# Weights of the feed-forward and of two layers in scaled float16 parts instead of float32r parts

## The chip, the cores and the metric

The kernel runs on one core of one Trainium2 chip. The metric is the device time of one launch in microseconds, the median of several launches. Five engines matter: TensorE (PE) multiplies, its stationary operand being loaded by a separate step (PEld); VectorE (DVE) and ScalarE (ACT) work elementwise and are the ones that read TensorE's results out of PSUM; GpSimd (POOL) does small statistics; SyncE (SP) issues most DMAs. Each runs its own instructions in order and waits for the others on semaphores.

## The reference, cut to what matters

One decoder block over 512 tokens of width 1024, then two mixer layers over the same tokens and 256 context tokens, all in float32:

```python
h = rms_norm(x, norm_ffn_g)                       # end of the first block
x = x + jnp.square(jax.nn.relu(h @ w_ff1)) @ w_ff2

for i in range(2):                                # the two layers
    hx = rms_norm_2(x, g_pre) * (1.0 + scale_x) + shift_x
    hc = rms_norm_2(ctx, g_pre) * (1.0 + scale_c) + shift_c
    ... = in_proj(hx, w_in), in_proj(hc, w_in)    # 7200 columns
    ya = window_attn_latent(...)                  # branch a
    yb = mla_attn_latent(...)                     # branch b, over w_qb and w_kvb
    yc = short_gated_conv(...)                    # branch c
    m = (sigmoid(ga) * ((ya * silu(za)) @ w_branch[0])
       + sigmoid(gb) * ((yb * silu(zb)) @ w_branch[1])
       + sigmoid(gc) * ((yc * silu(zc)) @ w_branch[2]))
    x = x + gate_x * rms_norm_2(m @ w_o, g_post)
```

Ahead of the feed-forward the first block has a projection, a sparse attention with compressed keys, a spatial gating unit and a cross attention to 256 memory tokens; this is called the front here.

## The kernel before

Precision comes from two parts. Each float32 operand is split into a high part in float32r and a low part (the rest, also float32r), and a product is made as three matmuls in `mm3` (L291 to L293): high by high, high by low, low by high, added up in PSUM. The moving operand has up to 512 columns.

Weights go through `Stream` (L147 on). SyncE loads chunks of 1024 columns into three rotating raw tiles; a chunk is two units of 512 columns; for each unit ScalarE writes the high part `wh` (L182) and VectorE the low part `wl` (L183) into a ring of nine such units. `pump` makes the next unit whenever the ring has room; `get` makes it at once if a product needs it. The ring is refilled as products release units.

The program is a list of operations written out by hand: for each product a block of weights (`wblk`) and a generator that yields its cost after each step. A driver (`tick`) runs them in order, pumps the ring, lets chains of dependent steps (norms, rotations, transposes) go on when their time is due, and mixes background attention in at a fixed rate. The framework then orders each engine's instructions.

`form_a` multiplies with tokens on the output partitions (weights move), `form_b` and the first feed-forward product with features on the output partitions (tokens move, 512 columns for x, 256 for the context). The stages, with their start in the profile:

- 0 us: the front. Its last part is w_mo's product and two blocks of modulation weights (`mod`).
- about 457: the feed-forward in eight chunks of 512 hidden columns, `ff1` and `ff2`; blocks of modulation weights stand between some.
- about 843: layer 0. Products KA and QA, then branch a's attention in the background of branch c's products (`conv`: CC, UC, BC, ZC).
- about 1105: KL and QL, then branch b's attention. ZA's products, the gate of branch a in pieces (`agate`), stand ahead of it and between its items as fillers.
- about 1349: `merge`, four steps for each branch in the order c, a, b; a step multiplies by its gate's weights and by w_branch. `zgate` (ZB, branch b's gate) stands ahead of b's merge. Then w_o.
- about 1768: layer 1, the same without context outputs.

Branch values go to DRAM and come back (`y_load`), each split into float32r parts. Norms take six small steps on POOL (`rstd`, L279 to L287). In branch attention the probabilities and values are float16 or bfloat16 parts already.

## Time and profile before

| | |
|---|---|
| Three launches | 2448.72, 2451.61, 2451.70 us; median 2451.61 |
| Span of the profiled execution, first to last instruction | 2444.0 us |
| Matmuls in it | 14268, listed busy 2352.0 us |
| VectorE, ScalarE, POOL busy | 1458.1, 1123.3, 208.7 us |
| Mean granted TensorE clock | 0.988 of full |

The profile is of one execution; its span leaves out what lies around the instructions of the program, and that execution's own launch time is not listed beside it. A matmul's listed duration includes its pipeline's tail, which overlaps the next matmul; the spacing of starts is what each costs in a stream. Half clock was granted only in a dozen short stretches, most in the front and at the starts of the stages.

### The profile page before, as it was taken

To read this page: it belongs to the slowest core of one execution; us is meant where nothing else is said; L and a number is where in the kernel's file an instruction comes from. 1 tells how busy PE (TensorE), PEld (TensorE's weight loads), DVE (VectorE), ACT (ScalarE), POOL (GpSimd) and SP (SyncE) were. 2 spreads that over 40 slices of the span, in tenths; PEclk is the share of its full clock that TensorE was granted. 3 is DMA by queue.
4 is the path that set the end of the run, shared out by engine and by line. 5 is a ranking of instruction groups with operands and counts; after the bars stand their busy time and mean duration, and the time that the engine had idled before them with its cause. 6 is when DMAs were issued, how large, how long until landed. Compare 5 with 4: busy or idle time off the path is not lost. (4 is left out here: it accounts for less than half of the span.)

```text
span 2444.0 us, 37374 instructions
## 1 busy us (share of the span) xinstructions
PE 2352.0 (96%) x14268; PEld 1971.2 (81%) x14268; DVE 1458.1 (60%) x2772; ACT 1123.3 (46%) x2461; POOL 208.7 (9%) x574
## 2 busy tenths in 40 slices
PE   7899899999999999999999999999989999999998
PEld 6777687777788888889888888888878798888886
DVE  5878668655544667664677423443577657863444
ACT  5656457543333345434576322322445556752332
POOL 4310321200000100003000000000400020000001
PEclk9999999999999999999999999999999999999999
DMA  4512445533532311212212321222422223133332
GB/s 156 131 54 70 156 129 171 150 121 121 164 104 86 121 52 46 63 36 62 80 49 78 119 61 54 81 70 78 137 79 61 63 61 107 44 109 90 104 95 95
DMA packets 182247, 226.63 MB, mean 93 GB/s; under 512 B 28588, under 2 KB 130908, under 8 KB 182068
## 3 DMA queue, kind: packets, MB, share of 16 engines
q1 hardware_dynamic: 158116, 187.67, 25.8%
q10 hardware_dynamic: 23952, 36.57, 4.5%
q8 instruction: 112, 1.84, 0.3%
q14 instruction: 67, 0.55, 0.1%
HBM read 207.33 MB, written 16.88 MB: 92 GB/s over the span
## 5 line engine op out<-in xcount | busy, mean ns | idle before, releaser
L182 ACT ACTIVATE wh<-raw 128x512 fp32r<-128x512 f32 (+4 forms) x668 | 401.8, 618 | 454.3 <-PE mm L292 223.6
L183 DVE TENSOR_TENSOR wl<-raw,wh 128x512 fp32r<-128x512 f32 (+4 forms) x668 | 437.7, 673 | 201.7 <-ACT wh L182 194.1
L291 PE MATMUL mm<-hTh,wh 128*128 128x512 f32 (+1 forms) x1040 | 415.2, 400 | 2.0 <-ACT wh L182 1.2
L292 PE MATMUL mm<-hTl,wh 128*128 128x512 f32 (+1 forms) x1040 | 410.6, 395 | 0.0
L293 PE MATMUL mm<-hTh,wl 128*128 128x512 f32 (+1 forms) x1040 | 409.5, 394 | 0.0
L293 PEld LDWEIGHTS mm<-hTh,wl 128*128 128x128 f32 x1040 | 196.3, 189 | 45.1
L291 PEld LDWEIGHTS mm<-hTh,wh 128*128 128x128 f32 x1040 | 196.5, 189 | 44.7 <-ACT wh L182 1.6
L292 PEld LDWEIGHTS mm<-hTl,wh 128*128 128x128 f32 x1040 | 196.8, 189 | 40.9
L568 ACT ACTIVATE ph<-mm 128x512 f16<-128x512 f32 (+2 forms) x300 | 147.7, 503 | 148.9 <-PE mm L564 132.7
L569 DVE SCALAR_TENSOR_TENSOR pl<-mm,ph 128x512 f16<-128x512 f32 (+2 forms) x300 | 166.9, 567 | 73.7 <-ACT ph L568 70.5
L291 PE MATMUL mm<-wh,hTh 128*128 128x512 f32 (+4 forms) x512 | 186.4, 366 | 4.6 <-ACT wh L182 1.9
L293 PE MATMUL mm<-wh,hTl 128*128 128x512 f32 (+4 forms) x512 | 185.3, 362 | 0.0
L292 PE MATMUL mm<-wl,hTh 128*128 128x512 f32 (+4 forms) x512 | 184.9, 363 | 0.0
L564 PE MATMUL mm<-ident,P 128*128 128x128 f32 x928 | 148.8, 278 | 3.7 <-ACT P L551 1.8
L279 POOL TENSOR_SCALAR s<-s 128x1 f32<-128x1 f32 (+4 forms) x89 | 35.4, 397 | 1116.5 <-ACT xn L444 949.1
L551 ACT ACTIVATE P<-S,s 128x768 f32<-128x768 f32 (+4 forms) x160 | 106.0, 667 | 30.1 <-PE mm L564 16.3
L564 PEld LDWEIGHTS mm<-ident,P 128*128 128x128 f32 x928 | 106.4, 142 | 14.9 <-ACT P L551 3.6
L1897 ACT ACTIVATE z<-mm 128x256 f32<-128x256 f32 (+1 forms) x72 | 37.4, 519 | 170.1 <-PE mm L293 170.1
L291 PEld LDWEIGHTS mm<-wh,hTh 128*128 128x128 f32 x512 | 98.0, 192 | 17.2 <-ACT wh L182 2.3
L291 PE MATMUL mm<-hch,wh 128*128 128x256 f32 x384 | 110.8, 289 | 0.5 <-DVE y L1646 0.4
L1904 DVE SCALAR_TENSOR_TENSOR z<-z,mm 128x512 f32<-128x512 f32 (+1 forms) x48 | 28.8, 599 | 134.7 <-PE mm L293 134.4
L293 PE MATMUL mm<-hch,wl 128*128 128x256 f32 x384 | 109.0, 284 | 0.0
(473 smaller groups left out, 5347.2 us busy)
## 6 DMA issues: line engine op xcount, KB each, us to landing
raw<-in_w_in_dram SPq DMA_DIRECT2D x124, 512.0 KB, 3.7
raw<-in_w_ff_dram SPq DMA_DIRECT2D x64, 512.0 KB, 3.9
raw<-in_w_mod_dram SPq DMA_DIRECT2D x48, 512.0 KB, 3.8
raw<-in_w_branch_dram SPq DMA_DIRECT2D x24, 512.0 KB, 3.3
raw<-in_w_o_dram SPq DMA_DIRECT2D x16, 512.0 KB, 3.8
raw<-in_cmp_w_dram SPq DMA_DIRECT2D x16, 256.0 KB, 3.6
raw<-in_w_out_dram SPq DMA_DIRECT2D x8, 512.0 KB, 4.4
raw<-in_w_mkv_dram SPq DMA_DIRECT2D x8, 512.0 KB, 4.8
```

The lines of the kernel that those rows point to most:

```text
L182: nc.scalar.activation(hi[:, :m], src, AF.Copy)
L183: nc.vector.tensor_sub(lo[:, :m], src, hi[:, :m].bitcast(FT))
L279: POOL.tensor_scalar(a, ms, EPS, None, op0=OP.add)
L291: PE.matmul(ps, ah, bh, start=start, stop=False)
L292: PE.matmul(ps, ah, bl, start=False, stop=False)
L293: PE.matmul(ps, al, bh, start=False, stop=stop)
L551: ACT.activation(P, v[:, j, :], AF.Exp, bias=it.nb[:, j:j + 1], accum_out=it.den[:, j:j + 1])
L564: PE.transpose(ps[:, a - a0, :], it.P[0 if len(it.P) == 1 else j][:, c:c + 128], ident)
L568: ACT.activation(ph[:, :m], ps[:, :m], AF.Copy, scale=PSC)
L569: DVE.scalar_tensor_tensor(pl[:, :m], ps[:, :m], PSC, ph[:, :m], op0=OP.mult, op1=OP.subtract)
L1897: ACT.activation(th[sg], ps, AF.Tanh, scale=0.5)
L1904: DVE.scalar_tensor_tensor(th[sg], th[sg], 1.0, ps, op0=OP.add, op1=OP.mult)
```

## The change

All weight products of the feed-forward and, in the layers, those of w_in and w_branch take two float16 parts instead of two float32r parts; the number of matmuls of these products and their shapes stay. The front, the modulation weights, w_qb, w_kvb and w_o keep float32r (`fr=True`). Float16 has a narrow range, so:

- Weights get a scale for each group of blocks (a feed-forward step's two blocks, a gate with its w_branch, two of conv's blocks, or a single block). `stat` squares each raw chunk on ScalarE with its sums kept, up to four chunks ahead; `scale` and `total` add the sums over partitions by a one-column matmul and take the power -0.5 on POOL. Only then can a group's parts be made.
- A unit is now 1024 columns, the ring still nine units. The high part is a scaled copy on ScalarE, or on POOL where `pool=True` (conv, KL, QL, ZA); the low part is one VectorE instruction for each 512 columns, emitted one pump later (`finish`).
- Norm gains and the layers' scale and shift are scaled once, branch values by a scale from their own squares (`ystat`, `yscale`); the products are multiplied back where they leave PSUM (`unscale`, argument `c` or `u`).
- The token tiles `hTh`, `hTl` become two halves each. After the memory query product float16 tiles take the first halves and the second halves become four more raw tiles; two more come from the space of memory attention's output. So there are three raw tiles in the front and nine after.
- The last ZA block's pieces (two in layer 0, one in layer 1) move from branch b's attention to the start of `merge`; ZB moves from ahead of b's merge to ahead of a's. Branch b's gated values stay on the chip until they are split.

```diff
 class Stream:
...
+    def stat(self, lo):
...
+        for a in range(0, m, w):
+            b = min(m, a + w)
+            nc.scalar.activation(lo[:, :b - a], t[:, a:b], AF.Square, accum_out=g.t[:, g.cols:g.cols + 1])
...
+        if g.seen == g.total:
+            self.full.append((self.state.clk, g))
...
+    def pump(self, must=False):
...
+        while self.full and self.full[0][0] + LAG <= self.state.clk:
+            self.scale()
...
+        n = 1 if self.ns < 4 else 2
+        while n and self.nstat < self.nd and self.nstat <= ci + AHEAD:
+            n -= self.stat(lo)
...
+        elif fr:
             nc.scalar.activation(hi[:, :m], src, AF.Copy)
             nc.vector.tensor_sub(lo[:, :m], src, hi[:, :m].bitcast(FT))
         else:
...
+            s = g.t[:, G_S:G_S + 1]
+            if u.blk.pool:
+                nc.gpsimd.tensor_scalar(hi[:, :m], src, s, 1.0, op0=OP.mult, op1=OP.mult)
+            else:
+                nc.scalar.activation(hi[:, :m], src, AF.Copy, scale=s)
...
+    def finish(self):
...
+            for a in range(0, l.shape[-1], 512):
+                b = slice(a, min(a + 512, l.shape[-1]))
+                self.nc.vector.scalar_tensor_tensor(l[:, b], src[:, b], s, h[:, b], op0=OP.mult, op1=OP.subtract)
...
+    def total(ss, s, i):
+        b = sbp.tile([128, 2], BF, tag="sb", name="sb")[:, 0:1]
+        with nc.allow_low_precision(reason="a scale need not be exact"):
+            DVE.reduce_sum(b, ss, axis=AX)
+        ps = trtile(1)
+        PE.matmul(ps[:, 0, 0:1], onesb.to_broadcast([128, 128]), b, start=True, stop=True)
+        DVE.tensor_scalar(i, ps[:, 0, 0:1], 2.0 ** -30, 1e-30, op0=OP.mult, op1=OP.max)
+        POOL.tensor_tensor(s, i, neghalf[:, 0:1], op=OP.pow)
+        DVE.reciprocal(i, s)
...
+    def hT16():
+        for i, p in enumerate("hl"):
+            H[p] = one.tile([128, 8, 512], F16, tag=f"H{p}0", name=f"hT{p}")
+            more_raw(f"H{p}1")
...
         for n, b in enumerate((2, 0, 1)):
             if n == 0:
                 add(lambda: yc_load(nn))
-            elif n == 2:
+                for n2 in range(behind, len(pieces)):
+                    f, sg = pieces[n2]
+                    add(lambda *b, n2=n2: piece(n2), *([za[f]] if sg == segs[0] else []))
+                add(lambda: ya_load(nn))
+            elif n == 1:
+                g = Group()
                 for f2 in range(2):
                     add(lambda bl, f2=f2: zgate(f2, segs, bl, yb_d, nn),
-                        wblk(w[:, ZB + f2 * 256:ZB + (f2 + 1) * 256]))
+                        wblk(w[:, ZB + f2 * 256:ZB + (f2 + 1) * 256], g))
```

How this orders the engines, at three places. First TensorE at the start of the feed-forward: `ms` are the modulation's vectors, `xn` a normed token tile to be transposed, `sb` a group's sums, `hTh` and `hTl` the tokens' parts. Before:

```order
L1267 MATMUL mm<-wh,ms_616 34x512
L460 MATMUL S<-ident,xn 128x128 x8
L1268 MATMUL mm<-wl,ms_616 2x512
...
L291 MATMUL mm<-hTh,wh 128x256
L292 MATMUL mm<-hTl,wh 128x256
...
L1270 MATMUL mm<-wh,ms_616 34x512
...
L293 MATMUL mm<-hTh,wl 128x256
```

Now:

```order
L1447 MATMUL mm<-wh,ms_618 34x512
L430 LDWEIGHTS onesb
L430 MATMUL S<-sb,onesb 128x1
...
L416 LDWEIGHTS wh
L416 MATMUL mm<-hTh,wh 128x256
L417 LDWEIGHTS wh
L417 MATMUL mm<-hTl,wh 128x256
```

Each float16 matmul has its own load instruction, where a float32r matmul carries it within, and two sums over partitions stand ahead of the first product.

Second ScalarE at the same place: `z` is the first product on its way out, `raw` a chunk of weights, `gs` a group's sums and scale. Before:

```order
L182 ACTIVATE wh<-raw 128x512 x2
L296 ACTIVATE hTh<-S 128x4x128
L1215 ACTIVATE z<-mm 128x256 x2
L182 ACTIVATE wh<-raw 128x512
L1216 ACTIVATE z<-z 128x256 x2
```

Now:

```order
L421 ACTIVATE hTh<-S 128x4x128
L224 ACTIVATE wl,gs<-raw 128x1024
L1451 ACTIVATE z<-mm 2x512
L224 ACTIVATE wl,gs<-raw 128x1024
L273 ACTIVATE wh<-raw,gs 128x1024 x8
...
L224 ACTIVATE wl,gs<-raw 128x1024 x2
L1392 ACTIVATE z<-mm 128x256
```

Copies of 512 columns became a square (with the low part's tile as its scratch) and a scaled copy, of 1024 columns each.

Third POOL at the start of layer 0, where the six steps of `rstd` for x's token tiles stand (`s`). Before:

```order
L279 TENSOR_SCALAR s_8955<-s_8953 128x1
L281 TENSOR_TENSOR s_8957<-s_8955,nh 128x1
L283 TENSOR_TENSOR s_8959<-s_8957 128x1
L284 TENSOR_TENSOR s_8959<-s_8959,s_8955 128x1
L285 TENSOR_SCALAR s_8959<-s_8959 128x1
```

Now:

```order
L404 TENSOR_SCALAR s_8948<-s_8946 128x1
L406 TENSOR_TENSOR s_8950<-s_8948,nh 128x1
L271 TENSOR_SCALAR wh<-raw,gs 128x1024
L408 TENSOR_TENSOR s_8952<-s_8950 128x1
L271 TENSOR_SCALAR wh<-raw,gs 128x1024
L409 TENSOR_TENSOR s_8952<-s_8952,s_8948 128x1
L410 TENSOR_SCALAR s_8952<-s_8952 128x1
```

Copies of weights for conv now stand between the steps of a norm; one more stands ahead of the norm before it.

## Rows read from the trace of the kernel before

**Rows 1.** The page: span, and busy time, share and instructions by engine.
```profile
span 2444.0 us, 37374 instructions
PE 2352.0 (96%) x14268; PEld 1971.2 (81%) x14268; DVE 1458.1 (60%) x2772; ACT 1123.3 (46%) x2461; POOL 208.7 (9%) x574
```

**Rows 2.** Stretches: us, engines' busy us (instructions), granted clock, DMA share, GB/s.
```profile
0.00:457.00 457.00, 415.93 (x2996) 332.90 (x2997) 343.45 (x634) 271.53 (x619) 113.32 (x294) 0.97 0.41 125
457.00:843.00 386.00, 384.46 (x1747) 308.64 (x1747) 206.31 (x324) 150.90 (x260) 13.74 (x32) 1.00 0.39 123
843.00:1105.00 262.00, 255.58 (x1773) 221.94 (x1772) 167.10 (x399) 118.89 (x290) 1.95 (x7) 0.99 0.18 51
...
1349.00:1768.00 419.00, 415.95 (x2285) 358.42 (x2284) 167.01 (x260) 119.39 (x220) 26.49 (x63) 1.00 0.27 84
```

**Rows 3.** Timeline, TensorE, merge: start, duration, engine, line, operation; float32r.
```profile
1408.81 0.40 PE L291 MATMUL mm<-hTh,wh 128*128 128x512 f32 x1
...
1417.23 0.28 PE L291 MATMUL mm<-hch,wh 128*128 128x256 f32 x1
...
1420.08 0.28 PE L291 MATMUL mm<-yh,wh 128*128 128x256 f32 x1
```

**Rows 4.** Timeline, TensorE: first and last of two runs of 16-bit matmuls.
```profile
163.92 0.27 PE L983 MATMUL O<-Vd,ph 128*128 128x256 bf16 x1
...
164.91 0.27 PE L987 MATMUL O<-Vd,pl 128*128 128x256 bf16 x1
...
1343.66 0.22 PE L585 MATMUL O<-ph,vb 128*128 128x128 f16 x1 [0.48 <-DVE yb L1794]
...
1344.78 0.22 PE L585 MATMUL O<-ph,vb 128*128 128x128 f16 x1
```

**Rows 5.** Groups by line and shape: count, busy us, mean ns, idle before.
```profile
L182 ACT ACTIVATE wh<-raw 128x512 fp32r<-128x512 f32 x620 | 380.7, 630 | 434.6 <-PE mm L292 208.2 <-PE mm L293 82.2 <-DVE oc L1067 50.8
L551 ACT ACTIVATION_READ_ACCUMULATOR P<-S,s 128x1 f32 x160 | 32.6, 203 | 0.0
L444 ACT ACTIVATE xn<-oc 128x1024 f32<-128x1024 f32 x12 | 12.6, 1053 | 12.4 <-DVE oc L1067 10.8 <-POOL s L284 1.6
L183 DVE TENSOR_TENSOR wl<-raw,wh 128x512 fp32r<-128x512 f32 x620 | 415.5, 688 | 188.4 <-ACT wh L182 181.1 <-PE mm L564 4.7 <-PE mm L292 1.0
L539 DVE TENSOR_TENSOR nb<-s,sk 128x1 f32<-128x1 f32 x64 | 9.6, 151 | 0.6
L512 DVE SCALAR_TENSOR_TENSOR vb<-xn,s,vb 128x512 f16<-128x512 f32 x6 | 4.4, 747 | 0.1
L501 POOL TENSOR_TENSOR s<-s,nh 128x1 f32<-128x1 f32 x6 | 3.6, 607 | 206.5 <-DVE s L500 206.5
```

**Rows 6.** Groups by line and shape, POOL: its two widest kinds.
```profile
L876 POOL COPY Vd<-v 32x384 bf16<-32x384 bf16 x4 | 2.1, 525 | 17.6 <-DVE v L874 17.5
L1253 POOL MEMSET xn<- 128x1024 f32 x1 | 1.0, 952 | 0.0
```

**Rows 7.** Timeline, the first microseconds, VectorE and POOL.
```profile
7.70 0.22 POOL L279 TENSOR_SCALAR s<-s 128x1 f32<-128x1 f32 x1 [6.52 <-ACT xn L444]
...
9.70 1.28 DVE L448 SCALAR_TENSOR_TENSOR xn<-x,s,g 128x1024 f32<-128x1024 f32 x1 [2.71 <-POOL s L287]
9.75 1.31 POOL L279 TENSOR_SCALAR s<-s 128x1 f32<-128x1 f32 x1
```

**Rows 8.** Waits (total us, times, longest): feed-forward twice, then merge.
```profile
PE mm L291 <- ACT wh L182: 1.2, 1, 1.2
...
ACT wh L182 <- PE mm L293: 68.3, 10, 8.5
...
PE mm L291 <- ACT yh L296: 2.6, 1, 2.6
```

**Rows 9.** Timeline, TensorE at the start of layer 0.
```profile
843.14 1.06 PE L460 MATMUL S<-ident,xn 128*128 128x128 f32 x8
848.01 1.30 PE L460 MATMUL S<-ident,xn 128*128 128x128 f32 x5 [3.81 <-DVE xn L450]
```

More of the change, by code (lines that the diff above doesn't have):

```diff
@@ L157, in __init__ @@
         self.ns = 0
-        self.done = 0
+        self.nstat = 0
         self.live = 0
+        self.full = []
+        self.half = None
     def loads(self):
-        while self.nd < len(self.chunks) and self.nd - self.done < RAWB:
-            dmas, _ = self.chunks[self.nd]
-            t = self.rawp.tile([128, 1024], FT, tag="raw", name="raw")
+        while self.nd < len(self.chunks) and self.slots:
+            dmas, us = self.chunks[self.nd]
+            t = self.slots.pop(0)
             for dst, src in dmas:
@@ L275, in decoder_kernel @@
     POOL.memset(onesf, 1.0)
+    onesb = one.tile([128, 1], BF, tag="onesb", name="onesb")
+    POOL.memset(onesb, 1.0)
     def rstd(ms, n, p=128):
@@ L410, in decoder_kernel, with more_raw @@
     prevb = one.tile([128, 128], BF, tag="prevb", name="prevb")
[L412 to L413 removed]
+    H = {p: Halves(*[one.tile([128, 4, 512], FR, tag=f"H{p}{i}", name=f"hT{p}") for i in range(2)]) for p in "hl"}
+    def hT16():
+        for i, p in enumerate("hl"):
+            H[p] = one.tile([128, 8, 512], F16, tag=f"H{p}0", name=f"hT{p}")
+            more_raw(f"H{p}1")
+    def more_raw(tag):
+        t = one.tile([128, 2, 1024], FT, tag=tag, name="raw")
+        stream.slots += [t[:, 0], t[:, 1]]
+        stream.loads()
     def hA(t, k):
@@ L1330, in s23_start @@
         open_scope(f"s{i}")
+        rot["kd"] = Rot(sc["kd"], "kd", 2, 256)
         lay["i"] = i
+        lay["ih"] = f"l{i}"
+        lay["yss"] = [small(8) for _ in range(3)]
+        lay["yn"] = dict.fromkeys("abc", 0)
         one2 = sc["one"]
-        ra = one2.tile([128, 384], FT, tag="ra", name="ra")
+        ra = one2.tile([128, 384], FT, tag="yb", name="ra")
         nc.scalar.dma_start(out=ra, in_=c_ra)
@@ L2154, in decoder_kernel @@
     layer(1)
-    stream = Stream(nc, rawp, ringp, [b for blks, _ in ops for b in blks])
+    slots = [one.tile([128, 1024], FT, tag=f"raw{i}", name="raw") for i in range(3)]
+    stream = Stream(nc, slots, ringp, scalep, total, D, [b for blks, _ in ops for b in blks])
     stream.loads()
```

446 lines of the change are left out of this document (297 added, 149 removed).

## The prediction, made before the changed kernel ran

> **What bounds the kernel now.** I read the page's busy times first, then a table of stretches, then the spacing of matmuls in the timeline, then the waits. TensorE is busy 96% of the 2444.0 us span [rows 1]. That word needs care: a 128x512 matmul is listed with 0.39 to 0.40 us, but the next one starts after 0.23 us, so "busy" also covers a tail that overlaps its successor. What counts is the spacing. In a clean run of the merge stage 36 matmuls with 512 float32r columns start within 8.42 us, 233.9 ns apart, and the 24 with 256 columns behind them within 2.85 us, 118.8 ns apart [rows 3]. In the feed-forward stretch (386 us) and in the merge stretch (419 us) the matmuls simply follow one another; TensorE is busy all but 1.5 and 3 us there, VectorE and ScalarE about half the time or less [rows 2]. The waits say who leads: in the feed-forward ScalarE's split of weights waits 68.3 us for a matmul (a ring slot that is still being read), while matmuls wait 1.2 us for that split [rows 8]. Weights are ready ahead of their use, so in these stretches the time is the number of matmuls times their spacing. In the front (0 to 457) TensorE has 41 us without work, on chains of dependent steps; the change hardly enters there.
>
> **What float16 does to the spacing.** The trace of before has 16-bit matmuls, each with a load of its own 128x128 stationary tile as the changed ones will have: ten with 256 columns start within 0.99 us, 9 spacings of 110 ns, and 21 with 128 columns within 1.12 us, 20 of 56 ns [rows 4]. So 128 more columns cost 54 ns, and 512 columns come to 110 + 2 x 53 = 216 ns (estimate; twice the 256-column spacing gives 220, the longest). Against 233.9 that is 17.9 ns less for each matmul; for 256 columns 118.8 - 110 = 8.8, up to 9.7 with the rounding of the rows; I take 9.3. Per column both are 0.035, which gives 10 ns for 288 and 13.5 for 384 columns.
>
> The counts follow from the loops. Feed-forward: 8 chunks x (96 + 96) = 1536, of which 48 are split in two halves of 256 columns. Layer 0: 1584 with 512 columns (merge 864, conv 384, ZA 96, ZB 96, QA 144), the same number with 256 (context; KA for QA), 144 with 288, 144 with 384. Layer 1: 1536 with 512, 144 with 256, 144 with 288, 96 with 384. Together 4608 x 17.9 = 82.5, 1824 x 9.3 = 17.0, 288 x 10 = 2.9 and 240 x 13.5 = 3.2: **105.6 us less TensorE work.** Nothing in TensorE's work for the front, the attention products, the modulation, qb, kvb and w_o changes.
>
> **What it adds.**
> - On TensorE: 74 one-column products for sums (66 weight groups, 2 modulations, 6 branch sums). No row shows one; between nothing (it slips behind a wait) and the 56 ns of [rows 4], I take 56: 4.1 us.
> - On ScalarE, for each 1024 columns of weights: before, two copies of 630 ns; after, a square of 1053 with its sum (203) and one scaled copy of 1053 [rows 5], 1.05 us more. In the feed-forward 64 x 1.05 = 67 us on top of 150.9, 218 of some 359 us, 61%. It stays beside the matmuls and I cost it at nothing; without that cover it would be 67.
> - On VectorE the low parts: 2 x 747 (a scalar_tensor_tensor with float16 output) for 2 x 688 [rows 5], 0.12 us more for each chunk, 8 us in the feed-forward, plus some five small instructions of 0.15 for each group: nothing on the path, with 206 of 386 us busy there [rows 2].
> - At each group a chain: the last square's sum 0.20, a reduce 0.15, the product, a VectorE step 0.15, POOL's power 0.61, a reciprocal and the factor 0.3, the scaled copy 1.05, two low parts 1.49: some 4.0 us [rows 5]. The ring holds nine units of 1024 columns behind it (before: nine of 512), each worth some 24 matmuls x 216 ns = 5 us, and nine raw tiles stand for four chunks of a group. So it is hidden, except where a ring starts empty of scaled parts: ahead of the first feed-forward product, where four squares (4 x 1.26 = 5.0) come before the chain (4.0). Between 0 and 9 us; 4 taken, since slots for these loads open a whole attention earlier.
> - On POOL: high parts of conv, KL, QL and ZA, 27 chunks for each layer. No row shows POOL reading 1024 columns. A memset of 1024 takes 952 ns, a copy of 384 bfloat16 columns 525 ns [rows 6]; from 0.95 to 384-column pace x 1024 = 1.4 us, and twice that if its two operations are done one after the other: 1.4 taken, as the row that reads. Two things queue behind them. First the norms at the start of a layer: in the order on POOL a copy stands before x's norm and two more between steps of the next one. TensorE waits 3.81 us there for exactly such a norm [rows 9], so up to 3 x 1.4 = 4.2 for each layer; 4 taken, 8 in all. Second VectorE in conv: its low part now waits for a POOL copy instead of a ScalarE copy of 0.63, and attention's reductions are queued behind it. VectorE is busy 167 of 262 us there and TensorE has only 6 us without work [rows 2]. Between 0 and 16 chunks x 1.4 = 22 us a layer; 4 taken for each, 8 in all, nearer to none because VectorE has a third of its time free.
> - With one answer, nothing: the gains scaled once (two VectorE passes over 1024 columns, in the memory block), the factor on the way out of PSUM (the same instructions with another operand, one more on VectorE in branch c's merge), the squares of branch values on ScalarE (0.6 each beside matmuls), the narrower tiles of the front's compression, the same DMAs in number of bytes. Each hides beside matmuls on an engine with free time.
> - Moved: layer 0's two and layer 1's one last ZA piece go from branch b's attention to the start of merge, ahead of branch c's first use. TensorE waited 2.6 us there for yh [rows 8]; the pieces (24 x 216 and 24 x 110 ns, 7.8 us) cover that. Attention loses the same filler, about a wait of 1 us each. I take 2 us less for both layers together. ZB, moved one merge earlier, has its sum ready a whole merge ahead and costs nothing.
>
> **A rule against it.** A POOL instruction on one column that took 0.22 us at 7.70 lasts 1.31 us at 9.75, just as long as VectorE's two-input instruction that began at 9.70 [rows 7]. The Trainium skill ("SBUF — State Buffer", Who interferes with whom) states the rule: POOL and VectorE share a pair of ports under an exclusive lock, held for the whole instruction, when POOL reads SBUF and VectorE has two SBUF inputs. The trace agrees, and the rule speaks against this part of the change: it says that the new copies stop VectorE's low parts too. What that makes of the sum is the first rival.
>
> **Sum.** -105.6 + 4.1 + 4 + 8 + 8 - 2 = -83.5. The span falls from 2444.0 to 2360.5. Launches were timed at a median of 2451.61, 7.6 us above the profiled span; with the same 7.6 I get **2368 us**, 3.4% less. A measurement of this kernel can tell about 0.2% from no change, some 5 us.
>
> **Rivals.**
> 1. POOL and VectorE block one another in conv and the lat stage. Then each of the 54 copies costs up to its own 1.4 and the 0.69 of a low part it waits for, 2.1 x 54 = 113 us if all of it lay on the path. VectorE's free third says most does not; with a third exposed 38 us instead of my 16: 2390, and up to 2410. For it: [rows 7] and the norms at a layer's start. Against it: the ring's depth.
> 2. Everything added is hidden and the longer ring and nine raw tiles take up waits as well: -105.6 + 4.1 - 4 = -105.5, 2346; with 512 columns at 214 ns another 9 less, 2337. For it: TensorE barely waits for weights now [rows 8].
> 3. It doesn't do what it says at 512 columns: 16-bit matmuls of that width keep 234 ns, because what holds them is not the operand width. No 16-bit row has 512 columns. Then only the narrower ones gain, -23.1 + 22.1 = -1.0: 2451, no change. Against it: 56 and 110 ns lie on a straight line through nearly no fixed cost.
> 4. Slower: the group chain is not hidden. If units of a group become ready only after TensorE has used up the ring, each of 66 groups exposes 4.0 us, 264 us; it decides from 105.6 / 66 = 1.6 us exposed for each group, and in full gives 2444 - 105.6 + 264 + 22 + 7.6 = 2632. For it: no part can be made before the last chunk of its group has landed and been squared. Against it: the ScalarE waits of 68.3 us for slots [rows 8] show supply well ahead.
>
> **How the numbers follow.** Forecast (2355 to 2382) 0.66; rival 1 (2383 to 2415) 0.13; rival 2 (2335 to 2354) 0.12; rival 3 (2440 to 2456) 0.03; rival 4 (above 2457) 0.06. Faster 0.91, same 0.03, slower 0.06. The range takes the forecast, rival 2 and most of rival 1: 2337 to 2406.
>
> **What would show it.** In the changed profile: the spacing of 512-column matmuls in feed-forward and merge 214 to 218 ns (right) or 234 (rival 3); the feed-forward stretch about 386 - 27 = 359 us long; layer 0's merge, from 1349 to 1768, 26 us shorter but for the 7.8 us of the moved pieces; matmuls waiting for wh or wl hardly more than before (otherwise rival 4, with ScalarE's squares or POOL's power as releasers); POOL copies of wh near 1.4 us, and VectorE's waits for wh in conv short (long ones, and a conv stretch no shorter than 262 us: rival 1); at a layer's start TensorE's wait for the norm 4 us longer; at the start of merge no wait for the branch. I am wrong if TensorE's clock falls more often than before, or if ScalarE or VectorE is the one that TensorE waits for in the feed-forward.

## The result and the profile after

The changed kernel takes 2423.26 us (median of four launches, 2421.47 to 2425.71) against 2451.19 for the kernel before on the same chip: a ratio of 0.9886, 95% interval 0.9872 to 0.9900. It is faster by 28 us (1.1%), a third of the forecast 83.5, and the time lies above the forecast range. The profiled execution has a span of 2419.7 us, against 2444.0 in [rows 1].

The page of the changed kernel, span and busy time by engine:

```profile
span 2419.7 us, 38066 instructions
PE 2261.3 (93%) x14342; PEld 1505.2 (62%) x14342; DVE 1544.2 (64%) x3136; ACT 1298.1 (54%) x2745; POOL 320.7 (13%) x703
```

TensorE's busy time fell by 91 us, so its work did shrink; ScalarE gained 175 us and VectorE 86. The spacing of matmuls is what was forecast. The timeline of TensorE in layer 0's merge (start, duration, engine, line, operation):

```profile
1384.75 0.38 PE L416 MATMUL mm<-hTh,wh 128*128 128x512 f16 x1
...
1389.93 0.38 PE L416 MATMUL mm<-yhl,wh 128*128 128x512 f16 x1
...
1392.52 0.27 PE L416 MATMUL mm<-hc,wh 128*128 128x256 f16 x1
...
1395.14 0.27 PE L416 MATMUL mm<-yhl,wh 128*128 128x256 f16 x1
```

24 matmuls with 512 columns start within 5.18 us, then 12 within 2.59, both 215.8 ns each; 24 with 256 columns within 2.62, 109 ns each. The number of matmuls by width is as counted in the prediction, so some 105.6 us of TensorE work did go. Where the time came back shows in the stretches. First the kernel before, from the feed-forward on, then the changed kernel (length, then busy us and instructions of TensorE, its weight loads, VectorE, ScalarE and POOL, then the granted clock, the DMA share and GB/s). The four of before are the feed-forward, branch b's attention in layer 0, and layer 1's two stretches ahead of merge:

```profile
457.00:833.00 376.00, 374.46 (x1662) 298.71 (x1663) 197.17 (x312) 144.71 (x248) 11.28 (x25) 1.00 0.39 122
...
1109.00:1349.00 240.00, 228.54 (x1688) 206.53 (x1687) 167.08 (x351) 147.95 (x378) 22.29 (x74) 0.99 0.22 65
...
1761.00:1976.00 215.00, 201.73 (x1328) 167.17 (x1326) 151.58 (x338) 105.87 (x245) 11.56 (x28) 0.98 0.27 79
1976.00:2165.00 189.00, 182.47 (x1348) 162.24 (x1347) 141.28 (x296) 125.04 (x310) 18.51 (x62) 0.99 0.23 64
```

```profile
469.00:821.00 352.00, 347.81 (x1666) 162.80 (x1665) 213.92 (x394) 204.94 (x334) 21.18 (x39) 0.99 0.42 134
...
1090.00:1332.00 242.00, 219.22 (x1649) 176.61 (x1648) 170.92 (x382) 164.95 (x415) 30.86 (x85) 0.98 0.23 69
...
1726.00:1961.00 235.00, 194.02 (x1337) 126.19 (x1336) 174.05 (x389) 113.62 (x265) 51.73 (x66) 0.95 0.25 75
1961.00:2153.00 192.00, 177.31 (x1320) 140.59 (x1318) 143.90 (x326) 137.88 (x336) 27.13 (x73) 0.98 0.24 72
```

The feed-forward lost 24 us of 27 forecast, but it starts 12 us later (469 instead of 457). In branch b's attention TensorE is busy 9 us less, and the stretch is 2 us longer. In layer 1's first stretch it is busy 8 us less, and the stretch is 20 us longer. The same as a table, by the first matmul of each stage in the traces (us, the last stage up to its last matmul; "L0 a" is layer 0 to the end of branch a's attention and conv, "L0 b" branch b's attention, "merge" with w_o). The other rows are the experiments below:

| kernel | front | feed-forward | L0 a | L0 b | merge 0 | L1 a | L1 b | merge 1 |
|---|---|---|---|---|---|---|---|---|
| before | 456.9 | 375.8 | 276.8 | 239.4 | 411.9 | 215.2 | 188.7 | 271.2 |
| changed | 468.9 | 352.3 | 268.8 | 241.7 | 394.1 | 235.2 | 192.4 | 257.9 |
| constant scale, squares kept | 457.4 | 373.6 | 271.5 | 240.4 | 393.4 | 231.9 | 193.3 | 256.4 |
| constant scale, no squares | 454.2 | 362.8 | 267.4 | 232.2 | 389.4 | 224.4 | 184.2 | 256.3 |
| the same, units of 512 | 450.2 | 355.4 | 264.1 | 224.8 | 391.8 | 210.2 | 181.9 | 258.0 |
| the same, ring of eighteen | 453.4 | 362.8 | 266.7 | 233.9 | 390.9 | 227.5 | 187.2 | 257.9 |

The stages in which TensorE runs from one matmul to the next (merge) gained what was forecast: 17.8 us for layer 0, where 26 less the 7.8 of the moved pieces was expected. Of the stages with chains of dependent steps only layer 0's first gained, 8.0 us; the other three became 2 to 20 us longer.

### The profile page after: what moved, and what is told of

Same layout as the page of the kernel before. It is cut to its first block, busy times and chain, and to the rows that moved or that the text cites. A ratio compares the mean times of both kernels' runs of the same rounds, so it can differ in the third digit from the quotient of the medians.

```text
span 2419.7 us, 38066 instructions
## 1 busy us (share of the span) xinstructions
PE 2261.3 (93%) x14342; PEld 1505.2 (62%) x14342; DVE 1544.2 (64%) x3136; ACT 1298.1 (54%) x2745; POOL 320.7 (13%) x703
## 5 line engine op out<-in xcount | busy, mean ns | idle before, releaser
L416 PE MATMUL mm<-hTh,wh 128*128 128x512 f16 (+1 forms) x1040 | 392.6, 378 | 7.3 <-ACT wh L273 3.1
L291 DVE SCALAR_TENSOR_TENSOR wl<-raw,gs,wh 128x512 f16<-128x512 f32 (+2 forms) x420 | 296.6, 751 | 150.6 <-ACT wl L224 116.5
L417 PE MATMUL mm<-hTl,wh 128*128 128x512 f16 (+1 forms) x1040 | 392.4, 377 | 0.0
L418 PE MATMUL mm<-hTh,wl 128*128 128x512 f16 (+1 forms) x1040 | 391.2, 377 | 0.0
L224 ACT ACTIVATE wl<-raw 128x1024 f16<-128x1024 f32 (+3 forms) x242 | 222.9, 921 | 69.6 <-PE mm L417 37.3
L416 PEld LDWEIGHTS <-wh 128*128 128x128 f16 x1712 | 168.0, 98 | 147.4 <-issue 6.8
L417 PEld LDWEIGHTS <-wh 128*128 128x128 f16 x1712 | 168.0, 98 | 146.1 <-issue 9.6
L273 ACT ACTIVATE wh<-raw,gs 128x1024 f16<-128x1024 f32 x156 | 175.3, 1141 | 105.9 <-PE mm L417 83.0
L416 PE MATMUL mm<-wh,hTh 128*128 128x512 f32 (+5 forms) x512 | 181.7, 356 | 5.5 <-DVE vf L1589 2.0
L418 PE MATMUL mm<-wh,hTl 128*128 128x512 f32 (+5 forms) x512 | 180.1, 352 | 1.8 <-DVE hTl L422 1.7
L417 PE MATMUL mm<-wl,hTh 128*128 128x512 f32 (+5 forms) x512 | 180.1, 352 | 0.3 <-DVE wl L267 0.3
L271 POOL TENSOR_SCALAR wh<-raw,gs 128x1024 f16<-128x1024 f32 (+3 forms) x54 | 65.8, 1219 | 328.2 <-PE mm L417 209.9
```

What stands on the lines that cost most here:

```text
L224: nc.scalar.activation(lo[:, :b - a], t[:, a:b], AF.Square, accum_out=g.t[:, g.cols:g.cols + 1])
L273: nc.scalar.activation(hi[:, :m], src, AF.Copy, scale=s)
L291: self.nc.vector.scalar_tensor_tensor(l[:, b], src[:, b], s, h[:, b], op0=OP.mult, op1=OP.subtract)
L416: PE.matmul(ps, ah, bh, start=start, stop=False)
L417: PE.matmul(ps, ah, bl, start=False, stop=False)
L418: PE.matmul(ps, al, bh, start=False, stop=stop)
```

## What the waits say

TensorE's waits in branch b's attention of layer 0 (total us, times, longest), before and then changed:

```profile
PE S L291 <- ACT P L551: 3.2, 4, 1.4
```

```profile
PE S L416 <- ACT P L721: 12.1, 11, 2.5
```

A score waits for an exponential nine microseconds more. ScalarE's timeline in one of these waits shows what stood ahead of it:

```profile
1263.62 1.13 ACT L273 ACTIVATE wh<-raw,gs 128x1024 f16<-128x1024 f32 x1
...
1264.66 1.04 ACT L224 ACTIVATE wl<-raw 128x1024 f16<-128x1024 f32 x1
1265.61 0.19 ACT L224 ACTIVATION_READ_ACCUMULATOR wl<-raw 128x1 f32 x1
1265.70 0.61 ACT L1862 ACTIVATE qb<-y 128x512 fp32r<-128x512 f32 x1
1266.34 0.87 ACT L738 ACTIVATE ph<-mm 128x512 f16<-128x512 f32 x2
1267.10 0.91 ACT L721 ACTIVATE P<-S,s 128x768 f32<-128x768 f32 x1
```

A scaled copy of one chunk and the square of another, with its sum, take 2.1 us without a break (1263.62 to 1265.70), and the exponential P comes behind them. Not all of the 2.1 us is P's delay: it needs the largest score of each row, and VectorE takes that until 1264.94:

```profile
1263.99 0.95 DVE L705 TENSOR_REDUCE s<-S 128x1 f32<-128x768 f32 x1
```

From then on some 0.8 us of the square are left, and 1.4 us of `qb` and `ph`, which the square had held up as well. ScalarE is busy 165 of 242 us in this stretch, 68%, so there is room on average; but the engine runs its instructions in order, and here the weights' stand ahead of the exponential. What the changed kernel spends on scaled copies (L273, L271) and on statistics (L224) is in its groups by line and shape (count, busy us, mean ns, idle before):

```profile
L273 ACT ACTIVATE wh<-raw,gs 128x1024 f16<-128x1024 f32 x156 | 175.3, 1141 | 105.9 <-PE mm L417 83.0 <-POOL gs L432 22.6
L224 ACT ACTIVATE wl<-raw 128x1024 f16<-128x1024 f32 x164 | 171.5, 1046 | 61.0 <-PE mm L417 35.6 <-PE mm L418 12.6 <-DVE ffh L1394 5.3
L271 POOL TENSOR_SCALAR wh<-raw,gs 128x1024 f16<-128x1024 f32 x40 | 53.0, 1328 | 222.0 <-PE mm L417 127.6 <-PE mm L418 69.1 <-issue 24.4
L224 ACT ACTIVATION_READ_ACCUMULATOR wl<-raw 128x1 f32 x242 | 45.6, 188 | 0.0
L224 ACT ACTIVATE wl<-raw 128x512 fp32r<-128x512 f32 x64 | 39.7, 620 | 1.9 <-PE mm L417 1.7
```

A square also uses the low part's tile as scratch, so that VectorE's low part must wait for it. In branch b's attention of layer 0 that is not what costs; VectorE waited 0.7 us for squares there:

```profile
L291 DVE SCALAR_TENSOR_TENSOR wl<-raw,gs,wh 128x512 f16<-128x512 f32 x23 | 16.3, 746 | 1.9 <-POOL wh L271 1.2 <-ACT wl L224 0.7
```

The second place is the start of layer 1. VectorE, POOL and TensorE in the changed kernel:

```profile
1741.55 6.57 DVE L291 SCALAR_TENSOR_TENSOR wl<-raw,gs,wh 128x512 f16<-128x512 f32 x6
1748.04 0.20 DVE L311 TENSOR_SCALAR gs<-gs,ih 128x1 f32<-128x1 f32 x1
1748.17 1.40 DVE L291 SCALAR_TENSOR_TENSOR wl<-raw,gs,wh 128x512 f16<-128x512 f32 x2
1749.49 0.74 DVE L2196 SCALAR_TENSOR_TENSOR xt<-ob,s,xt 128x512 f32<-128x512 f32 x1
```

```profile
1741.42 0.19 POOL L410 TENSOR_SCALAR s<-s 128x1 f32<-128x1 f32 x1
1741.59 4.67 POOL L271 TENSOR_SCALAR wh<-raw,gs 128x1024 f16<-128x1024 f32 x3
1746.22 0.62 POOL L412 TENSOR_TENSOR s<-s,s 128x1 f32<-128x1 f32 x1
```

```profile
1750.80 0.69 PE L1581 MATMUL S<-ident,kd 128*128 128x128 f32 x2 [8.64 <-ACT kd L1556]
```

Eight low halves stand in a row ahead of `xt`, w_o's result going into x, on which the norms and, by the profile's waits, `kd` depend; TensorE stands still for 8.64 us. Six of the halves take 1.10 us each instead of the 0.70 of the last two, while POOL makes three copies. These copies also stand between the last two steps of the norm that `xt` needs (L410 and L412), so `xt` could not start before 1746.84: for the first 4.7 us either of the two would have held it, for the last 2.6 the low halves alone do. Four theories follow: statistics load ScalarE; the wait of a group for its scale bunches the parts; POOL and VectorE block one another; fillers were lost with the moved pieces.

## Experiments

All times are medians; each ratio is to the kernel before, run beside it on the same chip (2449.2, 2452.7, 2451.7, 2450.8, 2451.8 and 2450.1 us on the six chips). "Constant" kernels assume a weight scale of 1024, so they are right only for weights of about this size.

**The pieces put back.**

```diff
-        behind = len(pieces) - len(segs)
+        behind = len(pieces)
```

> The changed kernel with the last ZA pieces (two in layer 0, one in layer 1) put back into branch b's attention as fillers. Theory 'filler': branch b's attention is bound by its own chain of scores, exponentials and parts, so the pieces are free there and cost 7.8 + 7.8 + 5.2 = 21 us in merge: 2402 to 2408, the layer-0 attention stretch (242 us) hardly longer, merge 394 -> about 380. Theory 'work added to ScalarE, VectorE and POOL': the stretch has no room, so what merge gains attention loses: 2420 to 2428.

2458.4 us, ratio 1.0034 (1.0022 to 1.0047). The expectation counted layer 0's two pieces twice: they are the two segments of one block and cost 7.8 us together, so at most 13 us were to be won. Instead 35 were lost. L0 b grew by 13.7 us and L1 b by 10.7, and merge did not shrink. The move that the prediction put at 2 us is what kept the changed kernel below the one before.

**High parts on ScalarE.**

The same is done for conv, KL and QL.

```diff
-        za = [wblk(w[:, ZA + f * 128:ZA + (f + 1) * 128], pool=True) for f in range(4)]
+        za = [wblk(w[:, ZA + f * 128:ZA + (f + 1) * 128]) for f in range(4)]
```

> The changed kernel with all high parts on ScalarE, none on POOL. Theory 'POOL and VectorE block one another': without the POOL copies the low parts fall back from up to 1.1 us for 512 columns to 0.7 and the norms on POOL no longer stand behind copies; layer 1's first stretch (235 us) loses 8 us or more, the whole 10 to 15: about 2410. Theory 'ScalarE's load delays the chains': 54 copies of 1.14 us come on top of the squares, 5 to 15 us slower: 2428 to 2438.

2424.9 us, ratio 0.9900 (0.9868 to 0.9933): no difference to the changed kernel, so neither expectation held. At the start of layer 1 the wait for `kd` falls from 8.6 to 3.2 us, but one for a norm's `xn` takes 7.4. POOL's 54 copies, with VectorE's slower halves beside them, and 54 more copies on ScalarE cost the same here.

**Constant scale, squares kept.** Parts wait for no group; the sums go unused.

```diff
+    def fix(self, g):
+        g.t = self.scalep.tile([128, 16], FT, tag="gs", name="gs")
+        self.nc.vector.memset(g.t[:, G_S:G_S + 1], 1024.0)
+        self.nc.vector.memset(g.t[:, G_I:G_I + 1], 1.0 / 1024)
+        g.ready = True
...
-        if not (must or fr or g.ready) and g.seen == g.total:
-            return False
```

> The changed kernel with a constant weight scale of 1024 for each group, ready from the start; the squares on ScalarE are still made (their sums unused), but no sum over partitions, power or reciprocal, and no part waits for its group. Theory 'hold-up': parts that all become possible at one moment stand as a burst ahead of the norm chains at the starts of the feed-forward and of the layers; without it the feed-forward starts at 458 to 462 instead of 469 and layer 1's first stretch takes 215 to 222 us instead of 235: 2395 to 2403. Theory 'load': the squares themselves are what is late; 2418 to 2425.

2425.2 us, ratio 0.9898 (0.9872 to 0.9923). The first feed-forward product starts at 457 again, and the stage then takes 21 us more; the sum is no better. (The starts are not alike: here the first product comes ahead of transposes of the last norms, at 459.27 and 465.74, which it follows in the changed kernel.) The wait for a group's scale is not what costs.

**Constant scale, no squares.** As above, without the activation of `stat`.

```diff
-            nc.scalar.activation(lo[:, :b - a], t[:, a:b], AF.Square, accum_out=g.t[:, g.cols:g.cols + 1])
```

> As the run before, with the squares left out as well: no statistics of weights at all. Theory 'hold-up': 0 to 4 us faster than with the squares. Theory 'load' (1.25 us of ScalarE for each 1024 columns ahead of exponentials and norm steps): 15 us or more faster than with the squares, most of it in branch attention, where a score waits for an exponential.

2379.7 us, ratio 0.9710 (0.9687 to 0.9734): 45.5 us faster than with the squares on the same chip, with no other edit. ScalarE's busy time is lower by 212 us than in the changed kernel, and the wait for exponentials in branch b's attention falls from 12.1 to 7.5 us. Page and wait of this run:

```profile
PE 2249.7 (95%) x14276; PEld 1497.2 (63%) x14276; DVE 1525.0 (64%) x3070; ACT 1085.8 (46%) x2261; POOL 286.1 (12%) x637
```

```profile
PE S L412 <- ACT P L717: 7.5, 7, 1.7
```

By the table the squares cost 14 us up to the end of the feed-forward, 4.1 and 8.2 in layer 0's two stretches, 4 in its merge, 7.5 and 9.1 in layer 1's: 29 us in the stretches with attention, 18 outside them. This is the largest part of the miss. To 2449.2 less the 105.6 us of TensorE work, 2343.6, some 36 us are still missing; several of the next runs look for them.

**Three raw tiles.** Constant, no squares, the two `more_raw` calls out.

```diff
-            more_raw(f"H{p}1")
...
-    add(lambda: more_raw("HCl"))
```

> Constant scale without squares (2379.7 us, with nine raw tiles), and only the three raw tiles of the front throughout. Theory 'burst': with nine landed chunks and the ring free, parts of up to nine units are written one after another, ahead of the steps of the norms (VectorE wrote eleven low halves in a row, 8.2 us, at the start of layer 1); three raw tiles let them come at the pace of the loads: layer 1's first stretch 224 -> 213 to 216, the feed-forward with the stretch ahead of it 817 -> 805 to 810, in all 2355 to 2365. Theory 'wide units and POOL copies': the raw tiles don't matter, 2376 to 2384.

2386.2 us, ratio 0.9732 (0.9712 to 0.9752), a little slower, with intervals that overlap. The raw tiles are not to blame. Without them the feed-forward starts 12 us later and ends 5.7 later.

**Units of 512 columns.** Constant, no squares; a chunk is again two units, nine units in the ring, and a raw tile is given back after its second unit.

```diff
-    per = 2 * max(1, 512 // N) if fr else max(1, 1024 // N)
-    kk = per // 2 if fr else per
+    per = 2 * max(1, 512 // N)
+    kk = per // 2
```

> Constant scale without squares (2379.7 us), nine raw tiles, but units of 512 columns as in the kernel before (the ring holds nine of them, half the weights). Theory 'width': a scaled copy of 1.14 and two low halves of 0.69 in a row, each twice what stood there before, hold up exponentials and norms; half of it gives 2355 to 2365, most in branch b's attention. Theory 'burst': the ring's nine units bound a burst, so half the width halves it too, 2362 to 2370 with most of it at the layers' starts and none in attention. Neither: 2376 to 2384.

2347.2 us, ratio 0.9577 (0.9562 to 0.9593): 32.5 us faster than with wide units, more than either theory expected, and 105.5 below the kernel before, as much as the 105.6 us of TensorE work.

**The supply of before.** Three raw tiles, units of 512, all high parts on ScalarE (the edits of the high parts, the raw tiles and the units together, on the constant kernel without squares).

```diff
-            more_raw(f"H{p}1")
...
-    per = 2 * max(1, 512 // N) if fr else max(1, 1024 // N)
+    per = 2 * max(1, 512 // N)
...
-        add(lambda b: form_a(b, every, hcx, ev_kl, f"l{i}"), wblk(w[:, KL:KL + 288], pool=True))
+        add(lambda b: form_a(b, every, hcx, ev_kl, f"l{i}"), wblk(w[:, KL:KL + 288]))
```

> Constant scale without squares, three raw tiles, units of 512 columns, all high parts on ScalarE: the supply of the kernel before with float16 in place of float32r. If the squares, the bursts and POOL's copies are all that took the gain, only the 105.6 us of TensorE work and the moved pieces are left: 2342 to 2352. If float16 itself makes attention or the starts wait (faster products leave the chains bare): 2360 or more.

2356.1 us, ratio 0.9612 (0.9596 to 0.9628), between the two expectations and 96.6 below the kernel before. That is close to the whole gain, so what faster products themselves leave bare is small. Against the later run with nine raw tiles (2338.5) the three cost 16 us (0.0064 of 2451).

**A quarter of the squares.** The changed kernel, complete, its scales from 256 of 1024 columns.

```diff
-        m = sum(len(u.ks) for u in us) * us[0].n
+        m = sum(len(u.ks) for u in us) * us[0].n // 4
...
-        DVE.tensor_scalar(i, ps[:, 0, 0:1], 2.0 ** -30, 1e-30, op0=OP.mult, op1=OP.max)
+        DVE.tensor_scalar(i, ps[:, 0, 0:1], 2.0 ** -28, 1e-30, op0=OP.mult, op1=OP.max)
```

> The changed kernel with the squares taken over a quarter of each chunk's columns (256 instead of 1024; the sum counted four times), all else as it is: the wait of a group for its scale stays. Theory 'columns squared': three quarters of the 45 us that the squares cost come back, 2423 - 34 = 2389. Theory 'the number of instructions': each square still costs its start and its 0.19 us read of the sum, 2405 to 2415.

2398.5 us, ratio 0.9782 (0.9765 to 0.9798): 25 us of the 45 are back, between the two expectations. Columns and starts both count.

**Units of 512 in the changed kernel.** Squares, group scales and raw tiles stay; the edit is that of the units.

```diff
-    per = 2 * max(1, 512 // N) if fr else max(1, 1024 // N)
+    per = 2 * max(1, 512 // N)
```

> The changed kernel, complete, with units of 512 columns instead of 1024 and nothing else changed: squares, group scales and nine raw tiles stay. If width and squares each cost their own share (32.5 us and 45 us without the other), this gives 2423 - 32 = 2388 to 2396. If the squares alone fill ScalarE so that width no longer matters beside them: 2410 to 2424.

2396.2 us, ratio 0.9777 (0.9760 to 0.9794): 27 us faster than the changed kernel. The two costs add up almost freely:

| us | all columns squared | a quarter | none (constant scale) |
|---|---|---|---|
| units of 1024 | 2423.3 | 2398.5 | 2379.7 |
| units of 512 | 2396.2 | 2369.6 | 2347.2 |

**Less made ahead.** Constant, no squares, wide units; the pump stops at five.

```diff
-        if self.ns >= len(self.units) or self.live >= RING:
+        if self.ns >= len(self.units) or self.live >= (RING if must else 5):
```

> Constant scale without squares, units of 1024 columns (2379.7 us), but parts are made ahead only while fewer than five units stand in the ring, about the 4608 columns that nine units of 512 hold; a product that needs more still makes them itself. Theory 'amount ahead': a shorter supply ends the bursts before the norms, as narrow units did: 2350 to 2362. Theory 'size of one step': what holds up the chains is the single unit with its 1.14 us copy and two low halves in a row: 2376 to 2384. A ring too short for products of eight units would make it slower than 2384, with TensorE waiting for wl.

2379.7 us, ratio 0.9708 (0.9691 to 0.9725): nothing. At the start of layer 1 the framework put the low halves in the same rows as without the edit (4, then 11), so the run says that the driver's count does not decide, not that the ring doesn't: the ring still had nine slots.

**The pieces put back, ScalarE relieved.** Constant, no squares, units of 512; the edit is that of the first run.

```diff
-        behind = len(pieces) - len(segs)
+        behind = len(pieces)
```

> Constant scale without squares, units of 512 columns (2347.2 us), with the last ZA piece of each layer's branch b put back into attention. With the full squares that cost 35 us. Theory 'load': with ScalarE relieved the pieces fill waits again as in the kernel before, within 5 us: 2343 to 2352. Theory 'place': they stand wrongly there whatever the load (merge then begins bare, waiting for branch c's parts), 15 us or more slower: above 2362.

2380.5 us, ratio 0.9718 (0.9698 to 0.9738): 33 us slower than without, as under full load. It is the place and not the load. TensorE's wait for branch c's parts at the start of merge, with the pieces in attention and then with the pieces ahead of merge:

```profile
PE mm L413 <- ACT yhl L678: 10.6, 3, 7.5
```

```profile
PE mm L413 <- ACT yhl L678: 2.4, 2, 1.6
```

The branch values now need a sum, a scale and a split after attention's end, and the piece covers that. In attention its own 7.8 us lengthen L0 b by 12.8. The wait and this are the part of the 33 us that layer 0 shows; the rest is not taken apart.

**A version that takes its scales from the weights.** A quarter of the squares and units of 512: the edits of the two runs above together.

```diff
-        m = sum(len(u.ks) for u in us) * us[0].n
+        m = sum(len(u.ks) for u in us) * us[0].n // 4
...
-    per = 2 * max(1, 512 // N) if fr else max(1, 1024 // N)
+    per = 2 * max(1, 512 // N)
```

> The changed kernel with both costs lowered but the scales still taken from the weights: squares over a quarter of each chunk's columns, units of 512 columns. If the two add up: 2398.5 - 32 = 2363 to 2372, faster than both kernels by over 50 us. If what is left of the statistics (starts, sums, the wait of a group) already fills the room that width had opened: 2380 or more.

2369.6 us, ratio 0.9668 (0.9649 to 0.9686): 82 us faster than the kernel before and 54 faster than the changed one. A scale from all columns bounds every element; one from a sample doesn't, for weights of very uneven size.

**Why wide units cost 32 us.** Constant, no squares in all of these. First, low halves one at a time:

```diff
+        if self.half is not None and not must and self.first():
+            return False
```

> Constant scale without squares, units of 1024 columns (2379.7 us), but a pump that follows a high part writes only the first 512 low columns, and the next pump the second 512 and the next unit: in the order of the program no more weight work stands between two other steps than with units of 512, except for the high copy, still of 1024 columns. Theory 'pace' (twice the columns at each pump): most of the 32.5 us comes back, 2350 to 2360. Theory 'length of one instruction' (the 1.14 us copy): 2374 to 2384.

2383.1 us, ratio 0.9725 (0.9710 to 0.9740): nothing gained, and at layer 1's start the low halves stood in the same rows as before the edit. Then every step of a unit in halves (`first` writes the first half's low part and the second half's high part), and high parts alone as two instructions:

```diff
+    def first(self):
...
+        self.low(0)
+        self.high(u, h[:, 512:], src[:, 512:], s)
```

> Constant scale without squares, ring of nine units of 1024 columns as in the changed kernel (2379.7 us), but every step on a unit is done in halves as with units of 512: high part of the first half, then at the next pump low part of the first half and high part of the second, then low part of the second. Nothing longer than 512 columns is left on any engine; only the ring, the loads and what is ahead are those of 1024. Theory 'length of an instruction': 2345 to 2355, as with units of 512. Theory 'ring and order' (the ring holds twice the weights, and the framework lets their parts stand in longer rows ahead of the norms: 4 and then 12 low halves at the start of layer 1, against 2, 1, 2, 2, 1): 2372 to 2384.

```diff
+            for a in range(0, m, 512):
+                b = slice(a, min(a + 512, m))
...
+                    nc.scalar.activation(hi[:, b], src[:, b], AF.Copy, scale=s)
```

> The same ring, each high part as two instructions of 512 columns at once, and the low halves as they were. Theory 'length of an instruction': 2345 to 2358. Theory 'ring and order': 2374 to 2384. Between, if the framework fits exponentials and norm steps between the two halves only where the order leaves them side by side: 2360 to 2372.

2389.4 (0.9746, 0.9729 to 0.9763) and 2388.0 us (0.9740, 0.9721 to 0.9759): some 8 us slower than unsplit by the ratios, so length is not it. (Such edits alone move the time by 8 us, so a difference below that between two kernels here proves little.) Last, units of 512 with a ring of nine slots of 1024, two units in each:

```diff
+        if second:
+            hi, lo = (x[:, 512:] for x in self.ch[1])
+        else:
+            hi, lo = (self.ringp.tile([128, 512 if fr else 1024], FR if fr else F16, tag=n, name=n) for n in ("wh", "wl"))
```

> Constant scale without squares, units of 512 columns (2347.2 us with nine of them in the ring), and a ring of nine slots of 1024 columns, two units in each, so up to eighteen units. Theory 'amount in the ring': 2372 to 2390, all of the cost of wide units, and layer 1's first stretch 210 -> 220 to 226 with 4 and 12 low halves in a row at its start. Theory 'granularity of a unit' (a product waits for all of a wide unit): 2345 to 2355.

2391.1 us, ratio 0.9758 (0.9741 to 0.9775). The grain is that of the fast run and the time that of wide units, even 44 us more than with the small ring (0.9758 less 0.9577): what the ring has room for is the cost. That a product must wait for the whole of a wide unit is not: in both runs TensorE waits under 4 us in all for high and low parts. VectorE at the start of layer 1, with the large ring and then with nine units of 512:

```profile
1711.52 10.13 DVE L295 SCALAR_TENSOR_TENSOR wl<-raw,gs,wh 128x512 f16<-128x512 f32 x12
1721.58 0.68 DVE L429 TENSOR_TENSOR hc<-S,hc 128x512 f16<-128x512 f32 x1
```

```profile
1689.36 1.40 DVE L287 SCALAR_TENSOR_TENSOR wl<-raw,gs,wh 128x512 f16<-128x512 f32 x2
1690.85 1.28 DVE L615 SCALAR_TENSOR_TENSOR xn<-xt,s,g 128x1024 f32<-128x1024 f32 x1
1692.05 1.41 DVE L287 SCALAR_TENSOR_TENSOR wl<-raw,gs,wh 128x512 f16<-128x512 f32 x2
1693.38 0.68 DVE L419 TENSOR_TENSOR hc<-S,hc 128x512 f16<-128x512 f32 x1
```

With room in the ring twelve low halves, 10.1 us, stand ahead of the norm's last step `hc`; with less room only two stand in a row. TensorE's waits in that stretch, large ring and then small:

```profile
PE mm L425 <- DVE hc L429: 9.2, 1, 9.2
```

```profile
PE mm L415 <- DVE hc L419: 2.7, 1, 2.7
```

This one row is not all of it: with three raw tiles the row of eleven was gone and layer 1's first stretch still took 221.6 us. That the ring's room costs 32 us or more is shown by this one pair, with the same grain; how it divides among single waits is not, and no run has wide units in fewer slots.

**POOL's copies once more.** Constant, no squares, units of 512, and the version with a quarter, each with high parts on ScalarE:

```diff
-        add(lambda b: form_a(b, every, hcx, ev_kl, f"l{i}"), wblk(w[:, KL:KL + 288], pool=True))
+        add(lambda b: form_a(b, every, hcx, ev_kl, f"l{i}"), wblk(w[:, KL:KL + 288]))
```

> Constant scale without squares, units of 512 columns (2347.2 us), and all high parts on ScalarE instead of POOL for conv, KL, QL and ZA. With squares and wide units POOL's copies made no difference (2424.9 against 2423.3). If they cost something once ScalarE has room: 3 to 8 us faster, 2339 to 2344, in conv and at the layers' starts. If not: 2345 to 2351.

> The version with a quarter of the squares and units of 512 columns (2369.6 us), all high parts on ScalarE. As in the run before if POOL's copies are what holds the norms: 2362 to 2367. If ScalarE, with the squares on it, becomes late instead: 2371 to 2380.

2338.5 us (0.9548, 0.9532 to 0.9564), the fastest of all, and 2373.4 (0.9685, 0.9668 to 0.9703). Where ScalarE has room, POOL's copies cost some 7 us by the ratios (0.9577 less 0.9548; the intervals just touch, and the edit also changes the order, so this is weak); where the squares fill it, nothing.

## Why the prediction was wrong, step by step

- **TensorE's work: right.** Spacing 215.8 and 109 ns for 216 and 109.5 forecast, and the counts as forecast. Rival 3 is out, and in rival 2 the part with the raw tiles was right (below).
- **"It stays beside the matmuls and I cost it at nothing": wrong, 45 us.** The squares were costed in the feed-forward alone, by ScalarE's busy share (forecast 61%, measured 205 of 352 us, 58%: the share was right). But the same squares run ahead of exponentials and norm steps in attention and at the stages' starts, where the latency of ScalarE is on the path. The runs with and without squares show the cost stage by stage, 14 us of it up to the end of the feed-forward and the rest in the layers; the wait for P is one of its places.
- **The longer ring: wrong sign, 32 us.** The prediction had it as cover, and rival 2 as a gain. It lets the framework write parts earlier than needed, ahead of steps that TensorE waits for. This is seen at the start of layer 1; in the other stages the order is not shown. The nine raw tiles, named in the same breath, do help: some 6 us with the large ring, within the intervals, and 16 with the small.
- **The group chain (rival 4, and 4 us at the start): not what costs.** Without it the feed-forward started 11.5 us earlier and still ended 10 us later (831.0 against 821.2). TensorE's waits ahead of the first product, in the changed kernel, are these:

```profile
PE S L630 <- DVE hTl L422: 6.8, 2, 3.8
PE mm L416 <- ACT wh L273: 3.1, 1, 3.1
```

The 3.1 are the chain's (4 forecast). The 6.8 are the last norms', against 0.2 in the kernel before, and were not in the sum. Squares stand among their steps on ScalarE, but are not the whole of it: without squares 5.1 us of these waits are left, and 3.6 with units of 512.
- **POOL's copies, 16 us: too much.** A copy takes 1.33 us (1.4 forecast). VectorE's halves last 1.10 us beside three of them, instead of 0.70. That agrees with the rule of the Trainium skill ("SBUF — State Buffer", Who interferes with whom), by which a VectorE instruction with two SBUF inputs contends with a POOL instruction that reads SBUF. The price was far lower than the sum and rival 1 had it: 0 us beside the squares and some 7 without them.
- **Moved pieces, −2 us: the wrong wait.** Put back they cost 33 to 35. The prediction took the wait of 2.6 us for `yh`, in the kernel before, as what they cover; in the changed kernel that wait has a sum and a scale in front of it and would be 10.6. So the move covers the sum and scale of the branch values as well, which the prediction did not see.
- **The clock: a sign that came true.** The prediction named a clock that falls more often as a sign of being wrong, and had no term for it. The mean granted clock is 0.978 instead of 0.988. The last section shows that this is a part of what squares and ring cost.
- **The sum.** −105.6 forecast and found in the spacing; by the runs +45 for squares and +32 for the ring, both costed at nothing, and 0 for the wait of groups: −28, which is what was measured. That it closes to a microsecond is luck: in the 105.5 that are left without squares and wide units, nine raw tiles instead of three gain some 16 us and POOL's copies cost some 7. The terms that the prediction did cost (22 us of additions) were small beside the two that it let hide behind "nothing".

## What to carry to other kernels

A busy share says whether an engine can keep up, not whether it is on time: cost an added instruction in each stage by what it stands ahead of in its engine's order, above all where the same engine does the steps of a dependent chain. A deeper buffer for work made ahead is not free cover: if a framework may place that work as soon as a slot is open, a longer ring puts it ahead of the urgent steps, so try half the depth before adding (here: nine units of 512 columns instead of 1024). And a statistic that need not be exact can be taken from a sample: a quarter of the columns gave back more than half of its cost.

## What the runs showed of the hardware that was not expected

After a wait the clock costs a second time. The granted clock fell to half at 467.49, within the 3.06 us wait; behind that wait, at the feed-forward's start, float16 matmuls of 256 columns came 0.21 us apart, twice the 109 ns found in merge, which is the lower of the two clock levels, 1.2 GHz; the trace shows it up to 474.3 us:

```profile
468.87 0.39 PE L416 MATMUL mm<-hTh,wh 128*128 128x256 f16 x1 [3.06 <-ACT wh L273]
469.06 0.42 PE L417 MATMUL mm<-hTl,wh 128*128 128x256 f16 x1
469.27 0.42 PE L416 MATMUL mm<-hTh,wh 128*128 128x256 f16 x1
```

In layer 1's first stretch the granted clock went from 0.98 to 0.95; from the end of the 8.64 us wait to 1764.6 it was 0.50. How much this adds to waits can be read from pairs of runs with the same 14276 matmuls. Constant scale with squares kept (the page without squares stands above), then units of 512 with the ring of eighteen and with the ring of nine:

```profile
PE 2267.6 (93%) x14276; PEld 1510.1 (62%) x14276; DVE 1528.8 (63%) x3070; ACT 1298.8 (54%) x2745; POOL 283.6 (12%) x637
```

```profile
PE 2255.7 (94%) x14276; PEld 1504.5 (63%) x14276; DVE 1535.1 (64%) x3074; ACT 1114.6 (47%) x2417; POOL 308.1 (13%) x695
```

```profile
PE 2240.7 (96%) x14276; PEld 1493.1 (64%) x14276; DVE 1536.7 (66%) x3074; ACT 1123.1 (48%) x2417; POOL 312.1 (13%) x695
```

With squares (span 2425.9 us against 2378.8) TensorE is without work for 29 us more and busy 18 us longer with the same matmuls, at a mean clock of 0.974 against 0.983. With the large ring (2388.3 against 2344.5) it is 29 and 15 us, at 0.979 against 0.986. So more than a third of either cost is no wait but slower matmuls, which fits the lower clock. A one-column power on POOL that took 0.57 us at one place lasted 2.06 us at another, behind a two-input low half and norm step of VectorE (three raw tiles, start of layer 1):

```profile
1711.79 0.57 POOL L402 TENSOR_TENSOR s<-s,nh 128x1 f32<-128x1 f32 x1
...
1724.12 2.06 POOL L402 TENSOR_TENSOR s<-s,nh 128x1 f32<-128x1 f32 x1
```
